# The recurrence's value rows: mixed in time in the first main stage for both directions, and loaded mixed

## The chip, the core and the metric

The kernel runs on one core of a Trainium2 chip. The core has a matrix engine (PE, with its weight loads shown as PEld), a vector engine (DVE), a scalar engine (ACT), a general engine (POOL), a queue that issues transfers (SP) and 16 DMA engines between the chip's memory (HBM) and the core's own (SBUF). Matmuls write into PSUM, eight banks of 128 x 512 numbers. Each engine runs its own instructions in the order in which they stand in its stream, and waits for other engines by semaphores. The metric is the device time of one execution in microseconds. Before the change it is 2432.16 us, the median of three runs (2431.11 to 2433.72).

## The reference, cut to what matters

One layer of a diffusion backbone for 256 latent tokens and 256 context tokens of width 2048. A modulated norm is projected by `w_in`; a bidirectional recurrence (RWKV-7) and a convolution module run on parts of the projection; gates merge both; then come an output projection and 16 routed experts. What the change touches is the mixing in time of the recurrence's inputs:

```python
def _rwkv_direction(P, lp, d):
    ...
    z = z + lp['tok_mu'][d] * (_token_shift(z, direction) - z)
    r, k, v, zw, za = jnp.split(z, ...)
    ...
# in the scan, per token and head
    S = S * w_t - sa * (kk_t * a_t) + v_t^T k_t
# per direction
    bonus = jnp.sum(r * k * _heads(lp['r_k']), axis=-1, keepdims=True) * v
```

For each direction d the rows of r, k and v are a weighted mean of a token and its neighbour, the one before for d = 0 and the one after for d = 1, with a weight for each channel. The value rows v enter the state update and the bonus.

## The kernel before, in words

Tokens lie along the free dimension: 512 columns, 256 of context and then 256 of latents; channels lie on the 128 partitions. The recurrence's 16 heads are eight pairs of 128 channels, and each pair has two directions, so there are 16 units, each a pair in one direction.

The weights come from HBM in pieces of 128 x 512 (`split_w`): SP loads `wraw`, ACT rounds it into `whi`, POOL or DVE takes the rest `wlo`, and PE runs three matmuls (L221 to L223) for each 128 x 128 block. In the first main stage POOL and DVE take `wlo` in turns; in the recurrence's stage POOL takes all.

First main stage (about 165 to 543 us): for each pair, `win_block` projects k, v and r into a PSUM bank, and `out_k`, `out_v` or `out_r` takes it out. The blocks are woven with eight blocks of the convolution (`glu_block`), each with 30 DVE instructions of one tap (L463), with a layer norm after them, and with pieces of the modulation's matmuls. `out_k` copies its bank into a padded tile `P2` (`padded`, L365 to L371: two POOL memsets of the two borders, one ACT copy) of which there are two, then mixes for both directions (`mix`, L373 to L375: ACT scales by one minus the weight, DVE adds the weighted neighbour) and SP stores both results to `kd`. `out_r` does the same with one token stream. `out_v` (L432 to L435) copies the bank as it is and stores it to `vd`, one store.

Recurrence's stage (about 543 to 1320 us): `load_pair` loads the raw value rows of a pair into the padded tile `Pv` (one buffer, two POOL memsets, one load of 256 KB). `rwkv_dir` makes a unit in five segments; segments of up to five units are interleaved. Its first segment loads `km`, `kn`, `rm` and `lw`, and fills the tile `VK` (one buffer): every third block of 64 columns holds mixed value rows (L641 to L644: two ACT and two DVE instructions of 128 x 256), the others hold rows made from `kn` and `rm`. `scores` multiplies blocks of `KB` and `VK` on PE (L729), DVE masks the result into `AT` (L731) and `KM` (L734), `flip` transposes `VK` and `KB` on PE (L740). From `AT`, ACT makes `Ab` (four copies), and from that DVE starts a serial chain of small instructions (L781 to L808) that inverts a triangular block. Value rows are also read for the bonus (L706, L708). Beside the units, pieces of the gates' projections (the fills, L221 to L223 into a bank `big`) and of the modulation (L271) run on PE.

After that come the output projections (to about 1430 us) and the experts (to the end), which are read from HBM in tiles of 2 MB.

The order on each engine is set by a scheduler that places instructions by their priority (the order in the program, with an offset for the fills) and by its own estimate of times. So a change of one instruction moves others, on all engines.

Of the kernel before, what the change touches and what calls it, by code (L numbers as in the profile page):

```python
# [9 lines left out]
F32 = mybir.dt.float32  # L10
F32R = mybir.dt.float32r
AF = mybir.ActivationFunctionType
OP = mybir.AluOpType
# [7 lines left out]
NP = 8  # L21
# [107 lines left out]
def kernel(  # L129
# [6 lines left out]
    PE, DVE, ACT, POOL, SP = nc.tensor, nc.vector, nc.scalar, nc.gpsimd, nc.sync  # L136
# [3 lines left out]
    dram = ctx.enter_context(tc.tile_pool(name="dram", bufs=1, space=bass.MemoryType.DRAM))  # L140
# [4 lines left out]
    def act_copy(o, i, scale=1.0):  # L145
        return ACT.activation(o, i, AF.Copy, scale=scale)  # L146
# [9 lines left out]
    def vec(name, i, n=1):  # L156
        a = _VEC[name][0]
        return V[:, a + i:a + i + n]
# [14 lines left out]
    omu = drv[:, 0:50]  # L173
# [27 lines left out]
    ygd = dram.tile([128, NP, NT], F32, name="ygd")  # L201
    gdr = dram.tile([128, 2, KD, NT], F32, name="gdr")
    kd = dram.tile([128, NP, 2, 2, 512], F32, name="kd")
    vd = dram.tile([128, NP, 512], F32, name="vd")
    nd = dram.tile([NP, 2, 2, 4, 128], F32, name="nd")
    rd = dram.tile([128, NP, 2, NT], F32, name="rd")

# [154 lines left out]
    with tc.tile_pool(name="p1", bufs=1) as p1:  # L362
        if WB1:
            WPS[:] = [[wst] + WB, [p1] + WB1]
        def padded(p, both):  # L365
            n = 2 if both else 1
            P = p1.tile([128, n, 258], F32, name="P%d" % n, bufs=2)
            POOL.memset(P[:, :, 0:1], 0.0)
            POOL.memset(P[:, :, 257:258], 0.0)
            act_copy(P[:, :, 1:257], p.rearrange("p (s t) -> p s t", s=2)[:, 2 - n:2])  # L370
            return P  # L371

        def mix(o, P, d, om, mu):  # L373
            ACT.activation(o, P[:, :, 1:257], AF.Copy, scale=om)
            DVE.scalar_tensor_tensor(o, P[:, :, 2 * d:2 * d + 256], mu, o, op0=OP.mult, op1=OP.add)  # L375

        for d in range(2):
            P = padded(acc0[d], True)
# [51 lines left out]
            kfin.extend([put, get, fin])  # L430

        def out_v(p, acc):  # L432
            t = p1.tile([128, 512], F32, name="vs", bufs=2)
            act_copy(t, acc)
            SP.dma_start(vd[:, p], t)  # L435

        def out_r(p, acc):
            P = padded(acc, False)
# [56 lines left out]

        BIG[:] = ["big", "rw"]
        outs = (out_k, out_v, out_r)
        kfin = []

# [94 lines left out]
    pend, acc = [], [0.0, 1.0]  # L594
# [23 lines left out]
    def rt(name, tag, shape, dt=F32):  # L618
        return rw.tile([128] + list(shape), dt, name=name, tag=tag, bufs=BUF.get(tag, 1))

    def hs(h):
        return slice(64 * h, 64 * h + 64)

    def rwkv_dir(p, d, Pv, bonr, bon, INP):
        c8 = lambda x: x.rearrange("p (c t) -> p c t", t=64)
        cp2 = lambda x: x.rearrange("p (c b) t -> p c b t", b=2)
        i16 = d * 8 + p
        mui = lambda s: 24 * d + 8 * s + p
        mu = lambda s: (omu[:, mui(s):mui(s) + 1], vec("mu", mui(s)))
        VK = rt("VK", "VK", [24, 64])  # L630
        VKv = VK.rearrange("p (c b) t -> p c b t", b=6)
        KB = rt("KB", "KB", [16, 64])
# [4 lines left out]
        SP.dma_start(kn, kd[:, p, d, 1])  # L637
        rm = rt("rm", "rm", [256])
        SP.dma_start(rm, rd[:, p, d])
        om, mv = mu(2)  # L640
        for s in range(2):  # L641
            o = VK[:, 12 * s:12 * s + 12:3]
            ACT.activation(o, c8(Pv[:, s, 1:257]), AF.Copy, scale=om)
            DVE.scalar_tensor_tensor(o, c8(Pv[:, s, 2 * d:2 * d + 256]), mv, o, op0=OP.mult, op1=OP.add)  # L644
        lw = rt("lw", "lw", [2, 128])
        SP.dma_start(lw, lora[p, :, d])
        lwh = rt("lwh", "lwh", [2, 128], F32R)
# [126 lines left out]
        for z, r in quads:  # L774
# [7 lines left out]
                                 op0=OP.mult, op1=OP.add)  # L782
# [4 lines left out]
        for j in range(1, 15):  # L787
            n, m = j, 15 - j
            tmp = rt("tmp", "tmp", [2 * 56])[:, 0:2 * n * m]
            if d == 0:  # L790
# [3 lines left out]
                o = Nv[:, :, j + 1:16, 0:j]  # L794
            else:
# [3 lines left out]
                o = Nv[:, :, 0:j, j + 1:16]  # L799
# [28 lines left out]
        e, o = (0, 32) if d == 0 else (32, 0)  # L828
        pq = c8(bank("sb"))
        for cp, h, c, q in each():  # L830
            a, b, i = 64 * q + e, 64 * q + o, 2 * cp + h
# [7 lines left out]
        for cp, h, c, q in each():  # L839
            a, b, i = 64 * q + e, 64 * q + o, 2 * cp + h  # L840
# [24 lines left out]
        for i, c in enumerate(order):  # L865
            cp, b, j, sl_ = c // 2, c % 2, i % 2, 2 * (i // 2)
            q = 1 - b
            for h in range(2):
                hh_ = h if b == 0 else 1 - h
                tick(0.1)  # L870
                lhs, o = KN[hs(q), cp, hh_], PP[j][hs(hh_)]
# [8 lines left out]
        for j in range(2):  # L880
            DVE.tensor_tensor(PT[:, 2 - j:8 - j:2], PP[j][:, 2 - 2 * j:8 - 2 * j:2], id3, op=OP.add)
            o = RB[:, j::2] if d == 0 else RB[:, 3 - j::-2]
# [29 lines left out]
    INP = rw.tile([128, 16, 32], F32, name="INP")  # L912
    POOL.memset(INP, 0.0)

    def load_pair(p):
        gw = rt("gw", "gw", [128])
        SP.dma_start(gw, g2[:, 128 * p:128 * p + 128])
        bonr = rt("bonr", "bonr", [128])
        POOL.tensor_scalar(bonr, bones, vec("rk", p), -1.0, op0=OP.mult, op1=OP.mult)
        Pv = rt("Pv", "Pv", [2, 258])  # L920
        POOL.memset(Pv[:, :, 0:1], 0.0)
        POOL.memset(Pv[:, :, 257:258], 0.0)
        SP.dma_start(Pv[:, :, 1:257], vd[:, p].rearrange("p (s t) -> p s t", s=2))
        return dict(bon=rt("bon", "bon", [256]), gw=gw, bonr=bonr, Pv=Pv)

    yh, yl = slh, sll

# [6 lines left out]
    def group_norm(p, S):  # L934
        (y0, y1), b0 = S["y"], S["bon"]
        DVE.tensor_tensor(y0, y1, y0, op=OP.add)
        ys = y0
        if dbg is not None and stop == "rwkv":
            SP.dma_start(dbg["y"][p], ys)
            SP.dma_start(dbg["bon"][p], b0)  # L940
        pm = bank(GNB)
        PE.matmul(pm[:, 0:256], bones, ys, start=True, stop=True)
        DVE.scalar_tensor_tensor(ys, pm[:, 0:256], -1.0 / 64, ys, op0=OP.mult, op1=OP.add)
        sq = rt("ysq", "ys", [256])
        ACT.activation(sq, ys, AF.Square)
        PE.matmul(pm[:, 256:512], bones, sq, start=True, stop=True)
        ACT.activation(sq, pm[:, 256:512], AF.Sqrt, scale=1.0 / 64, bias=eps[:, 1:2])
        DVE.reciprocal(sq, sq)
        POOL.tensor_tensor(ys, ys, sq, op=OP.mult)
        DVE.scalar_tensor_tensor(ys, ys, vec("lng", p), b0, op0=OP.mult, op1=OP.add)  # L950
        PE.matmul(pm[:, 0:256], S["gw"], sgl, start=True, stop=True)
        DVE.scalar_tensor_tensor(ys, ys, vec("lnb", p), pm[:, 0:256], op0=OP.add, op1=OP.mult)
        if p < PD:
            SP.dma_start(ygd[:, p, :], ys)
        else:
            act_copy(yh[:, p], ys)
            POOL.tensor_tensor(yl[:, p], ys, yh[:, p], op=OP.subtract)
# [4 lines left out]
    gens = {}  # L962

    def seg(n, i):
        if i >= len(units):
            return
        p, d = units[i]
        if n == 1:
            if d == 0:
                S[p] = load_pair(p)  # L970
            q = S[p]
            gens[i] = rwkv_dir(p, d, q["Pv"], q["bonr"], q["bon"], INP)
        r = next(gens[i])
        if n == 5:
            y = r
            ys = rt("ys", "ys", [256])
            act_copy(ys, y)
            S[p].setdefault("y", []).append(ys)
            if d == 1:
                group_norm(p, S[p])  # L980

    with tc.high_priority(offset=-LOWP):
        for f in early:
            f()
    seg(1, 0)
    seg(2, 0)
    seg(1, 1)
    seg(3, 0)
    seg(2, 1)
# [61 lines left out]
    for k in range(KD):  # L1051
# [13 lines left out]
        with tc.issue_after(a.ins):  # L1065
            if k in XLD:
                q = slice(4 * XLD.index(k), 4 * XLD.index(k) + 4)
# [86 lines left out]
    for s in range(2):  # L1154
        for q in range(4):
            o = xk[:, s, 4 * q:4 * q + 4]
# [153 lines left out]
    for s in range(2):  # L1310
        t = slice(128 * s, 128 * s + 128)
# [70 lines left out]
```

## Time and profile before

The profiled execution took 2433.61 us, 2431.8 us of which is its span from the first to the last instruction; what lies around the span is 1.8 us. It is 1.45 us above the median of the three timed runs.

| engine | busy us in the span | share |
|---|---|---|
| PE | 2006.9 | 83% |
| PEld | 1415.9 | 58% |
| DVE | 1023.9 | 42% |
| ACT | 763.2 | 31% |
| POOL | 650.8 | 27% |

A share over the whole span hides the stages: in the last 1000 us the DMA engines are 0.96 busy with the experts' weights and the other engines wait for them; in the first main stage and the output projections PE is the busiest, and in the recurrence's stage DVE comes close to it. Whatever moves the start of the experts' stage moves the end by as much. A busy PE is not PE at its peak, and the column of the granted clock says at what speed it ran: 1.00 is 2.4 GHz, and a mean below that is a mixture with 1.2 GHz.

### The profile page before, as it was taken

To read this page: it belongs to the slowest core of one execution; us is meant where nothing else is said; L and a number is where in the kernel's file an instruction comes from. 1 tells how busy PE (TensorE), PEld (TensorE's weight loads), DVE (VectorE), ACT (ScalarE), POOL (GpSimd) and SP (SyncE) were. 2 spreads that over 40 slices of the span, in tenths; PEclk is the share of its full clock that TensorE was granted. 3 is DMA by queue.
4 is the path that set the end of the run, shared out by engine and by line. 5 is a ranking of instruction groups with operands and counts; after the bars stand their busy time and mean duration, and the time that the engine had idled before them with its cause. 6 is when DMAs were issued, how large, how long until landed. Compare 5 with 4: busy or idle time off the path is not lost.

```text
span 2431.8 us, 45085 instructions
## 1 busy us (share of the span) xinstructions
PE 2006.9 (83%) x18730; PEld 1415.9 (58%) x18730; DVE 1023.9 (42%) x2029; ACT 763.2 (31%) x1524; POOL 650.8 (27%) x690
## 2 busy tenths in 40 slices
PE   7998999996877989988798996877777777777765
PEld 3787888894755877767678994433333333333332
DVE  2337888426777787665601543211111111111112
ACT  3254333634545565556443541000000000000002
POOL 1342333336433545445445732000000000000002
PEclk9999999998778999999998998888889889888987
DMA  9958666665213334234256887999999999999995
GB/s 384 343 183 271 216 218 233 202 213 181 60 56 109 125 123 139 96 134 152 97 197 198 280 314 303 427 427 428 428 427 427 428 427 429 427 428 427 428 416 221
DMA packets 145932, 669.94 MB, mean 275 GB/s; under 512 B 17344, under 2 KB 40000, under 8 KB 108608
## 3 DMA queue, kind: packets, MB, share of 16 engines
q1 hardware_dynamic: 128208, 455.49, 50.9%
q10 hardware_dynamic: 17520, 211.58, 20.6%
q8 instruction: 147, 2.41, 0.4%
q14 instruction: 57, 0.47, 0.1%
HBM read 647.28 MB, written 19.73 MB: 274 GB/s over the span
## 4 chain that ended last, share of the span: by engine, by line
DMA 31%; PE 20%; DVE 6%; ACT 3%; POOL 2%; issue 2%; SPq 0%; ACTq 0%; DVEq 0%; POOLq 0%
DMA wx<-in_w_gu 18%; DMA wx<-in_w_dn 10%; PE big L1261 2%; PE rw L1224 2%; DMA wraw<-in_w_in 2%; PE p L1293 2%; DVE N L800 1%; PE rw L1253 1%; PE big L221 1%; PE big L223 1%; PE rw L223 1%; PE big L222 1%; PE rw L221 1%; PE rw L222 1%; POOL wlo L217 1%
## 5 line engine op out<-in xcount | busy, mean ns | idle before, releaser
L217 POOL TENSOR_TENSOR wlo<-wraw,whi 128x512 fp32r<-128x512 f32 x292 | 394.4, 1356 | 517.4 <-ACT whi L146 450.0
L1261 PE MATMUL big<-wx,xse 128*32 128x512 f32 x2048 | 300.1, 721 | 160.3 <-DMA wx<-in_w_gu 158.4
L146 ACT ACTIVATE whi<-wraw 128x512 fp32r<-128x512 f32 x428 | 263.4, 627 | 420.2 <-DMA wraw<-in_w_in 130.0
L221 PE MATMUL big<-hh,whi 128*128 128x256 f32 x912 | 272.7, 299 | 13.6 <-ACT whi L146 6.1
L223 PE MATMUL big<-hh,wlo 128*128 128x256 f32 x912 | 271.0, 298 | 10.1 <-POOL wlo L217 9.9
L1261 PEld LDWEIGHTS big<-wx,xse 128*32 128x32 f32 x2048 | 63.8, 121 | 358.9 <-DMA wx<-in_w_gu 183.6
L222 PE MATMUL big<-hl,whi 128*128 128x256 f32 x912 | 268.1, 294 | 0.0
L1237 POOL TENSOR_TENSOR r<-r 128x256 f32<-128x256 f32 x11 | 8.2, 747 | 922.0 <-ACT r L1233 921.6
L221 PEld LDWEIGHTS big<-hh,whi 128*128 128x128 f32 x912 | 181.7, 199 | 40.0 <-issue 17.7
L223 PEld LDWEIGHTS big<-hh,wlo 128*128 128x128 f32 x912 | 181.6, 199 | 23.2 <-POOL wlo L217 14.1
L1274 ACT ACTIVATE th<-big 128x256 f32<-128x256 f32 x16 | 6.1, 384 | 584.9 <-PE big L1261 472.5
L222 PEld LDWEIGHTS big<-hl,whi 128*128 128x128 f32 x912 | 182.1, 200 | 7.4 <-issue 5.8
L1275 DVE SCALAR_TENSOR_TENSOR th<-th,big 128x256 f32<-128x256 f32 x16 | 6.7, 421 | 408.0 <-ACT th L1274 408.0
L1228 DVE SCALAR_TENSOR_TENSOR x<-rw,modT,x 128x256 f32<-128x256 f32 x256 | 111.3, 479 | 142.1 <-PE rw L1224 142.0
L217 DVE TENSOR_TENSOR wlo<-wraw,whi 128x512 fp32r<-128x512 f32 x136 | 112.7, 834 | 131.0 <-ACT whi L146 122.7
L1224 PE MATMUL rw<-oT,ye 128*128 128x256 f32 x512 | 132.4, 403 | 32.5 <-ACT ye L146 31.7
L223 PE MATMUL rw<-hh,wlo 128*128 128x256 f32 x512 | 149.9, 294 | 6.8 <-POOL wlo L217 6.8
L221 PE MATMUL rw<-hh,whi 128*128 128x256 f32 x512 | 150.3, 296 | 1.5 <-ACT whi L146 1.1
L222 PE MATMUL rw<-hl,whi 128*128 128x256 f32 x512 | 149.0, 293 | 0.0
L463 DVE SCALAR_TENSOR_TENSOR cv<-up,hcw,cv 128x256 f32<-128x256 f32 x240 | 144.6, 608 | 9.5 <-ACT cv L461 2.8
L1224 PEld LDWEIGHTS rw<-oT,ye 128*128 128x128 f32 x512 | 95.2, 196 | 85.9 <-ACT ye L146 72.4
L1253 PEld LDWEIGHTS rw<-oh,xk 128*128 128x128 f32 x1024 | 123.2, 194 | 34.2 <-issue 29.1
(359 smaller groups left out, 3901.4 us busy)
## 6 DMA issues: line engine op xcount, KB each, us to landing
wx<-in_w_gu ACTq DMA_DIRECT2D x66, 2048.0 KB, 39.2
wx<-in_w_gu SPq DMA_DIRECT2D x61, 2048.0 KB, 39.3
wm<-in_w_mod SPq DMA_DIRECT2D x96, 1024.0 KB, 7.2
wraw<-in_w_in SPq DMA_DIRECT2D x300, 256.0 KB, 4.2
wx<-in_w_dn ACTq DMA_DIRECT2D x32, 2048.0 KB, 38.6
wx<-in_w_dn SPq DMA_DIRECT2D x31, 2048.0 KB, 38.1
wraw<-in_w_o SPq DMA_DIRECT2D x64, 256.0 KB, 6.1
wraw<-in_w_co SPq DMA_DIRECT2D x32, 256.0 KB, 3.0
```

The source lines that it names most:

```text
L146: return ACT.activation(o, i, AF.Copy, scale=scale)
L217: (POOL if LO[0] < LO[1] else DVE).tensor_tensor(lo, raw, hi, op=OP.subtract)
L221: PE.matmul(o, hi, xh, start=start, stop=False, skip_group_check=True)
L222: PE.matmul(o, hi, xl, start=False, stop=False, skip_group_check=True)
L223: PE.matmul(o, lo, xh, start=False, stop=stop, skip_group_check=True)
L463: DVE.scalar_tensor_tensor(o, up[:, :, j:j + 64], hcw[:, i * KC + j:i * KC + j + 1], o, op0=OP.mult, op1=OP.add)
L800: DVE.tensor_tensor(o, o, tv, op=OP.add)
L1224: PE.matmul(pq[:, 256 * q:256 * q + 256], y[:, 128 * q:128 * q + 128], oT, start=True, stop=True)
L1228: DVE.scalar_tensor_tensor(x, pq[:, 256 * q:256 * q + 256], modT[:, 5, k + q, 0:1], x, op0=OP.mult, op1=OP.add)
L1253: PE.matmul(pxs[:, k], xk[:, s, k], oh[:, s, e], start=(s == 0), stop=(s == 1))
L1261: PE.matmul(pg[32 * j:32 * j + 32, :], xs[:, k, :], w[:, a:a + 512], start=(k == 0), stop=(k == KD - 1))
L1293: PE.matmul(pd[32 * j:32 * j + 32, u], aT[:, 128 * b + 32 * j:128 * b + 32 * j + 32], w[:, 2 * j + b, u], start=(b == 0), stop=(b == 1))
```

## The change

`out_v` now does with the value rows what `out_k` does with the keys: it copies the bank into a padded tile `P2`, mixes for both directions and stores two tiles; `vd` has a place for each direction. `rwkv_dir` loads its direction's mixed rows into a tile `vm` (one buffer) after `rm`, and one ACT copy puts them into every third block of `VK`. The padded tile `Pv`, its memsets and its load are gone, and so are the two ACT and two DVE instructions of each unit.

```diff
-    vd = dram.tile([128, NP, 512], F32, name="vd")
+    vd = dram.tile([128, NP, 2, 512], F32, name="vd")
...
         def out_v(p, acc):
-            t = p1.tile([128, 512], F32, name="vs", bufs=2)
-            act_copy(t, acc)
-            SP.dma_start(vd[:, p], t)
+            P = padded(acc, True)
+            for d in range(2):
+                i = 24 * d + 16 + p
+                t = p1.tile([128, 512], F32, name="vs", bufs=2)
+                mix(t.rearrange("p (s t) -> p s t", s=2), P, d, omu[:, i:i + 1], vec("mu", i))
+                SP.dma_start(vd[:, p, d], t)
...
-    def rwkv_dir(p, d, Pv, bonr, bon, INP):
+    def rwkv_dir(p, d, bonr, bon, INP):
...
-        om, mv = mu(2)
-        for s in range(2):
-            o = VK[:, 12 * s:12 * s + 12:3]
-            ACT.activation(o, c8(Pv[:, s, 1:257]), AF.Copy, scale=om)
-            DVE.scalar_tensor_tensor(o, c8(Pv[:, s, 2 * d:2 * d + 256]), mv, o, op0=OP.mult, op1=OP.add)
+        vm = rt("vm", "vm", [512])
+        SP.dma_start(vm, vd[:, p, d])
+        act_copy(VK[:, 0::3], c8(vm))
...
-        Pv = rt("Pv", "Pv", [2, 258])
-        POOL.memset(Pv[:, :, 0:1], 0.0)
-        POOL.memset(Pv[:, :, 257:258], 0.0)
-        SP.dma_start(Pv[:, :, 1:257], vd[:, p].rearrange("p (s t) -> p s t", s=2))
-        return dict(bon=rt("bon", "bon", [256]), gw=gw, bonr=bonr, Pv=Pv)
+        return dict(bon=rt("bon", "bon", [256]), gw=gw, bonr=bonr)
```

The scheduler's order shows where it now puts these. Lines of the changed kernel are three higher than before up to the recurrence and a few lower behind it.

On SP at the start of the recurrence's stage, before (`gw` and `lw` are small weights, `Pv` the raw value rows, `km`, `kn`, `rm` the rows of unit 0):

```order
L917 DMA gw<-in_g 128x128
L923 DMA Pv<-vd 128x2x256
L635 DMA km<-kd 128x512
L637 DMA kn<-kd 128x512
L639 DMA rm<-rd 128x256
L646 DMA lw<-in_lora 128x256
```

and now:

```order
L916 DMA gw<-in_g 128x128
L636 DMA km<-kd 128x512
L638 DMA kn<-kd 128x512
L640 DMA rm<-rd 128x256
L642 DMA vm<-vd 128x512
L645 DMA lw<-in_lora 128x256
```

The value rows of the first unit are issued fourth of the four loads, where they were first.

On DVE in the middle of the recurrence's stage, before (around the unit whose value rows are mixed at about 850 us; `AT` are the masked scores of one unit, `INP` and `N` the start of its serial chain):

```order
L674 SCALAR_TENSOR_TENSOR Wp<-dp,C 128x520
L674 SCALAR_TENSOR_TENSOR Wy<-di,C 128x520
L682 SCALAR_TENSOR_TENSOR Wy<-di,Wy 128x520
L731 TENSOR_TENSOR AT<-rw,C 128x4x64 x2
L644 SCALAR_TENSOR_TENSOR VK<-Pv,V,VK 128x4x64 x2
L692 TENSOR_TENSOR KB<-kp,Wy 128x4x2x64
L692 TENSOR_TENSOR KB<-ta,Wy 128x4x128
L781 SCALAR_TENSOR_TENSOR INP<-Ab,C 128x8x16
```

and now, at the start of the chain of a unit at the same place:

```order
L821 TENSOR_TENSOR T_9464<-T,sb 128x256
L823 STREAM_TRANSPOSE TT<-T_9464 128x256
L730 TENSOR_TENSOR AT<-rw,C 128x4x64 x2
L780 SCALAR_TENSOR_TENSOR INP<-Ab,C 128x8x16
L782 SCALAR_TENSOR_TENSOR INP<-Ab,C,INP 128x8x16
```

The pair of mixing instructions between the masked scores and the start of the chain is gone, and here the two `KB` products stand elsewhere too.

On DVE in the first main stage, now (`vs` are mixed value rows, `cv` the convolution's taps, `wlo` the rest of a weight piece); before, the two rows with `vs` were not there:

```order
L466 SCALAR_TENSOR_TENSOR cv<-up,hcw,cv 128x256 x5
L375 SCALAR_TENSOR_TENSOR vs<-P_2567,V,vs 128x512
L466 SCALAR_TENSOR_TENSOR cv<-up,hcw,cv 128x256
L375 SCALAR_TENSOR_TENSOR vs<-P_2567,V,vs 128x512
L466 SCALAR_TENSOR_TENSOR cv<-up,hcw,cv 128x256 x3
L217 TENSOR_TENSOR wlo<-wraw,whi 128x512
```

The mixing stands in the middle of a convolution's chain of taps.

## Rows read from the trace of the kernel before

**Rows 1.** Busy time of the engines by stretch, granted clock, DMA.

```profile
core 0: us, PE busy (x) PEld busy (x) DVE busy (x) ACT busy (x) POOL busy (x), PEclk, DMA share, GB/s
...
200.00:440.00 240.00, 222.65 (x1726) 196.57 (x1724) 201.01 (x343) 95.38 (x169) 81.10 (x87) 0.96 0.68 229
440.00:543.00 103.00, 99.97 (x811) 92.52 (x810) 35.01 (x59) 49.09 (x94) 33.38 (x33) 0.97 0.67 219
...
580.00:820.00 240.00, 186.31 (x2756) 152.84 (x2752) 183.07 (x346) 121.49 (x262) 106.78 (x126) 0.79 0.26 82
820.00:1060.00 240.00, 220.24 (x3301) 177.82 (x3301) 171.12 (x356) 145.30 (x314) 118.59 (x130) 0.95 0.41 135
...
1240.00:1320.00 80.00, 67.81 (x489) 58.79 (x488) 6.44 (x11) 30.56 (x58) 44.75 (x37) 0.87 0.65 208
1320.00:1430.00 110.00, 106.72 (x910) 103.52 (x911) 55.00 (x77) 56.54 (x108) 66.69 (x65) 1.00 0.82 279
```

**Rows 2.** Waits of the engines from 200 to 440 us: total, times, longest.

```profile
POOL up L456 <- DVE cv L463: 20.3, 6, 7.1
```

**Rows 3.** Waits of the SP queue, same stretch.

```profile
SPq L214 <- DVE wlo L217: 68.6, 36, 6.2
...
SPq L401 <- DVE km L375: 7.6, 4, 3.2
```

**Rows 4.** The mixing's DVE line: duration in ns, min/median/max, first and last start.

```profile
L375 DVE SCALAR_TENSOR_TENSOR km<-P,V,km x16: 735/745/1186, 160.0 to 516.4; 128x512 f32<-128x512 f32 x16
```

**Rows 5.** The mixing's ACT line, same columns.

```profile
L374 ACT ACTIVATE km<-P,drv x16: 709/715/733, 159.2 to 515.6; 128x512 f32<-128x512 f32 x16
```

**Rows 6.** The page's line of ACT's plain copy of 128 x 512.

```profile
L146 ACT ACTIVATE whi<-wraw 128x512 fp32r<-128x512 f32 x428 | 263.4, 627 | 420.2 <-DMA wraw<-in_w_in 130.0
```

**Rows 7.** What reads or writes the tile Pv.

```profile
L643 ACT ACTIVATE VK<-Pv,drv x32: 492/497/512, 546.8 to 1144.4; 128x256 f32<-128x256 f32 x32
L644 DVE SCALAR_TENSOR_TENSOR VK<-Pv,V,VK x32: 472/774/1396, 547.4 to 1145.0; 128x256 f32<-128x256 f32 x32
...
DMA to landing us min/median/max: 3.2/3.5/7.2
```

**Rows 8.** DVE's timeline: value rows followed by a wait (start us, us).

```profile
575.74 1.13 DVE L644 SCALAR_TENSOR_TENSOR VK<-Pv,V,VK 128x256 f32<-128x256 f32 x2
578.30 0.92 DVE L781 SCALAR_TENSOR_TENSOR INP<-Ab,C 128x128 f32<-128x128 f32 x1 [1.43 <-ACT Ab L146]
...
1144.57 0.87 DVE L644 SCALAR_TENSOR_TENSOR VK<-Pv,V,VK 128x256 f32<-128x256 f32 x2
1147.23 0.93 DVE L781 SCALAR_TENSOR_TENSOR INP<-Ab,C 128x128 f32<-128x128 f32 x1 [1.79 <-ACT Ab L146]
```

**Rows 9.** DVE's timeline: value rows with no wait behind them.

```profile
655.43 2.15 DVE L644 SCALAR_TENSOR_TENSOR VK<-Pv,V,VK 128x256 f32<-128x256 f32 x2
...
850.05 2.16 DVE L644 SCALAR_TENSOR_TENSOR VK<-Pv,V,VK 128x256 f32<-128x256 f32 x2
...
854.37 0.81 DVE L781 SCALAR_TENSOR_TENSOR INP<-Ab,C 128x128 f32<-128x128 f32 x1
...
962.98 1.80 DVE L644 SCALAR_TENSOR_TENSOR VK<-Pv,V,VK 128x256 f32<-128x256 f32 x2 [0.18 <-ACT VK L643]
```

**Rows 10.** ACT's timeline at the same place as the middle rows of that.

```profile
850.41 1.68 ACT L146 ACTIVATE Ab<-AT 32x256 f32<-32x256 f32 x4
```

**Rows 11.** SP's timeline at the start of the recurrence's stage.

```profile
543.05 0.43 SPq L923 DMA_DIRECT2D Pv<-vd  x1
543.52 0.47 SPq L635 DMA_DIRECT2D km<-kd  x1
...
544.63 0.43 SPq L639 DMA_DIRECT2D rm<-rd  x1
```

**Rows 12.** ACT's timeline there.

```profile
546.81 0.91 ACT L643 ACTIVATE VK<-Pv,drv 128x256 f32<-128x256 f32 x2 [2.52 <-DMA Pv<-vd]
```

More of the change, by code (lines that the diff above doesn't have):

```diff
@@ L627, in rwkv_dir @@
         i16 = d * 8 + p
-        mui = lambda s: 24 * d + 8 * s + p
-        mu = lambda s: (omu[:, mui(s):mui(s) + 1], vec("mu", mui(s)))
         VK = rt("VK", "VK", [24, 64])
@@ L971, in seg @@
             q = S[p]
-            gens[i] = rwkv_dir(p, d, q["Pv"], q["bonr"], q["bon"], INP)
+            gens[i] = rwkv_dir(p, d, q["bonr"], q["bon"], INP)
         r = next(gens[i])
```

## The prediction

> **What bounds the kernel now.** I read first the busy time by stretch, to see which stages the change touches and who is short there; then the waits of the first main stage; then the instructions that are removed and those like the added ones; and last the timelines of DVE, ACT and SP at the places where the removed ones stood.
>
> The stretches [rows 1] show three regimes. From 200 to 440 us, where the convolution's taps run, PE is busy for 222.7 of 240 us at a clock of 0.96, and DVE for 201.0 of 240, or 84%. From 440 to 543 us PE is busy for 100.0 of 103 and DVE for only 35.0. In the recurrence's stage DVE is busy for 183.1 of 240 us in the first part (580 to 820 us), while PE stands at 186.3 with a clock of 0.79; in the second part (820 to 1060 us) PE has 220.2 of 240 at 0.95 and DVE 171.1. So the first part belongs to the serial chain over DVE, ACT and PE, and in the second PE is close to being the limit. What lies behind (the output projections at a clock of 1.00, then the experts' weights) is not touched, and passes on what comes before it.
>
> The change moves work from the stage in which DVE sets the pace half of the time to one in which PE sets it. The question is how much of what goes was on the path, and how much of what comes finds room.
>
> **The first main stage: added.** Eight pairs of heads, two directions each: 16 DVE instructions of 745 ns [rows 4] are 11.9 us, 16 ACT instructions of 715 ns [rows 5] are 11.4 us; the copy out of the bank stays, 16 small memsets and eight more stores come. ACT is busy for 40% and 48% of the two stretches [rows 1] and hides its part. Of DVE's, the value rows of pairs 0 and 1 come before the taps begin, those of pairs 5 to 7 in the stretch with DVE at a third; PE's work covers them. Those of pairs 2, 3 and 4 are 6 x 0.745 = 4.5 us in the stretch that is 84% full. There DVE does reach PE: POOL stands 20.3 us at a memset that waits for taps [rows 2] with weight splits queued behind it, and SP stands 68.6 us at loads whose buffer DVE's half of the splits has not released [rows 3]. I take 4.5 x 0.84 = **+3.8 us**. The low end is 0: nothing goes from this stage that could gain. The high end adds SP: a store of mixed rows waits for DVE, and a key store did so for 7.6 / 4 = 1.9 us [rows 3] with weight loads queued behind it; six such stores are 11.4 us, together 15.9 us.
>
> **The recurrence's stage: its start.** The first unit's value rows were issued at 543.05 us, and ACT waited 2.5 us for them before it did anything else [rows 11, 12]. Now they go fourth, where `rm` went at 544.63 [rows 11], 1.6 us later; the copy behind is 0.28 us shorter (next part). On ACT the rounding of `lw` and the unit's first activations are queued behind it: **+1.3 us**, between 0 and that.
>
> **DVE's part, removed.** 32 instructions, of 472 to 1396 ns [rows 7]. After the first unit there are 15 pairs. In seven, DVE waits afterwards for something else, mostly for `Ab` from ACT, 1.43 us in the first and 1.79 us in the last of them [rows 8]: these are worth nothing. In eight pairs DVE goes on without a wait, from 655.43 to 962.98 us [rows 9]. There the pair takes up to 2.16 us, but a pair that nothing disturbs takes 0.87 [rows 8]. Of the time as it stands, less what the next wait would give back (at 850 us `Ab` is ready at 852.1 [rows 10] and the chain starts at 854.4 [rows 9], so all 2.16 count), the eight make 11.8 us; undisturbed they make 8 x 0.87 = 7.0 us. I take the lower, since what stretches a pair is still there when the pair is gone and meets the next instruction: **-7.0 us**, between 0 and -11.8.
>
> The Trainium skill (GPSIMD Engine Reference, "Specifications" and "Key points") says that POOL shares its SBUF interface with VectorE and that they contend when VectorE has two SBUF inputs. The mixing instruction has two such inputs, and so has the `KB` product behind it. By that rule the time over 0.87 us belongs to POOL's work, which stays, and the gain would be 7.0; without it, 11.8. The spread of one shape from 472 to 1396 ns agrees with it [rows 7].
>
> **ACT's part.** Two copies of 128 x 256, 0.91 us as a pair [rows 12], become one of 128 x 512; the nearest row is a plain copy of that size from SBUF, 627 ns [rows 6], so 0.28 us less for each unit. It counts where the chain waits for `Ab` behind it, five of the seven places above: **-1.4 us**, between 0 and 16 x 0.28 = -4.5.
>
> **Loads, POOL, the end of the stage.** A unit's load of 256 KB lands in 3.5 us [rows 7]; there are 16 for 8, in a stage whose DMA share is 0.26 to 0.41 [rows 1]. The buffer is free as soon as the copy before has run, a unit earlier than it is needed: nothing, as long as SP comes to it in time (a rival). 16 memsets on POOL go: nothing. The scheduler has also moved fills: behind the last unit's group norm 78 groups of three matmuls of gates stood before, 71 now. From 1240 to 1320 us 489 matmuls took 80 us [rows 1], 0.164 us each, so 21 fewer are **-3.4 us**; the low end is 0, since the seven stand inside the recurrence now.
>
> **Sum:** 3.8 + 1.3 - 7.0 - 1.4 - 3.4 = -6.7 us. On the profiled execution of 2433.6 that is 2426.9; this execution lies 1.45 us above the median of the timed runs, so I forecast 2425.5 us.
>
> **Rivals.**
> - *No change, PE paces it.* Four of the eight pairs lie after 820 us, where PE is 92% busy at 0.95 [rows 1]; DVE's freed time there is spent waiting for PE, and fills put forward cost what they save at the end. Then 3.8 + 1.3 - 3.5 - 1.4 = +0.2, or 2432.4. For it speaks that row; against it that this clock still leaves gaps, which a shorter chain fills.
> - *Slower, SP's queue in the first stage.* The stores of mixed value rows stand in front of weight loads. The high end: 15.9 + 1.3 - 7.0 - 1.4 = +8.8, or 2441.0. It decides once PE's idle time from 200 to 440 us, now 17.4 us, grows by more than the 10.5 us that the rest gives, to about 28. For it speaks SP's 68.6 us; against it that SP waits for buffers most of that time anyway, so that a store's wait partly lies in the same time.
> - *Slower, the mixed rows come late.* If SP, standing at other waits, issues `vm` only when `VK` is free, ACT stands up to 3.5 us with `Ab` queued behind: at five places 17.5, so 17.5 + 3.8 + 1.3 - 7.0 = +15.6, or 2447.8. Against it: a whole unit of cover.
> - *Faster than forecast.* The disturbed time goes too: -11.8 in place of -7.0, so -11.5, or 2420.7.
>
> **How the numbers follow.** Forecast 0.33, faster still 0.12, no change 0.30, SP's queue 0.19, late rows 0.06. A change of less than 0.2% (4.9 us) can't be told from none here; so faster 0.45, within 0.2% 0.30, slower 0.25. With the best ends of all terms (-11.8 - 4.5 - 3.4 = -19.7) the time would be 2412.5, with the worst 2449. The range is 2414 to 2441: it reaches past the larger gain below and to SP's price above, and leaves out the late rows and the rims. The forecast's own range, with the DVE term between -3.5 and -11.8, is 2420 to 2429. That the scheduler orders everything anew is in no term; it is why the range is not narrower.
>
> **What would show it.** Right: DVE from 200 to 440 us at about 205 us and the start of the recurrence's stage about 4 us later than 543; the copy into `VK` at about 0.63 us with no wait for a load except in the first unit; DVE's line of the value rows gone from the recurrence's stage, the eight chains starting a good 0.8 us earlier after `AT`; that stage about 10 us shorter. Wrong: the recurrence's stage as long as before with PE's busy time up in its second half (no change); SP's waits at stores of `vd` of 10 us and more, with PE idle from 200 to 440 us (slower); waits of ACT for `vm` (late rows).

## The result, and the profile after

The changed kernel took 2469.41 us, the median of 4 runs (2463.76 to 2474.34); the kernel before took 2431.64 us beside it (4 runs, 2423.98 to 2433.72). The ratio is 1.0156, 95% interval 1.0134 to 1.0178: slower by 38 us, outside the predicted range. The profiled execution of the changed kernel has a span of 2466.5 us, against 2431.8.

The same stretches as in [rows 1], after:

```profile
200.00:440.00 240.00, 223.57 (x1716) 192.20 (x1717) 209.75 (x353) 102.94 (x181) 83.46 (x95) 0.97 0.71 236
440.00:543.00 103.00, 97.81 (x818) 90.12 (x817) 41.35 (x66) 52.76 (x101) 34.42 (x39) 1.00 0.70 227
580.00:820.00 240.00, 191.26 (x2835) 158.61 (x2833) 167.96 (x356) 126.65 (x269) 102.69 (x119) 0.79 0.27 84
820.00:1060.00 240.00, 195.35 (x2947) 161.14 (x2947) 135.25 (x294) 118.77 (x257) 101.15 (x101) 0.86 0.34 108
1060.00:1240.00 180.00, 150.31 (x2061) 121.54 (x2060) 109.82 (x221) 94.61 (x200) 87.55 (x85) 0.91 0.40 131
1240.00:1320.00 80.00, 68.16 (x820) 56.42 (x819) 9.24 (x16) 35.13 (x74) 41.61 (x35) 0.96 0.62 205
1320.00:1430.00 110.00, 101.69 (x808) 98.71 (x809) 44.90 (x63) 52.57 (x99) 73.22 (x67) 0.94 0.76 238
```

Read it against [rows 1] line by line; the line that is not shown there, for the kernel before, is

```profile
1060.00:1240.00 180.00, 152.74 (x2249) 125.42 (x2245) 97.80 (x204) 89.12 (x195) 80.84 (x75) 0.91 0.37 122
```

The two lines of the first main stage are those of before but for DVE, which has 8.7 and 6.3 us more to do, and ACT, which has 7.6 and 3.7; PE does 2534 matmuls there where it did 2537. From 580 to 820 us the changed kernel is as good as before. Most of the loss stands in one line, 820 to 1060 us: PE did 2947 matmuls where it did 3301, its clock is 0.86 instead of 0.95, and every other engine did less too. From 1060 to 1240 us it did another 188 fewer. From 1240 us on PE makes up for work left behind (820 matmuls for 489).

What the change itself was to do, it did. Two groups of rows of the changed kernel, by tile: the mixing in the first stage (durations in ns, min/median/max, then first and last start), and the copy into `VK`:

```profile
L374 ACT ACTIVATE vs<-P,drv x16: 707/717/727, 163.7 to 530.2; 128x512 f32<-128x512 f32 x16
L375 DVE SCALAR_TENSOR_TENSOR vs<-P,V,vs x16: 741/747/1822, 164.5 to 531.1; 128x512 f32<-128x512 f32 x16
...
L146 ACT ACTIVATE VK<-vm x16: 613/632/634, 548.4 to 1181.0; 128x512 f32<-128x512 f32 x16
```

The waits of the SP queue in the recurrence's stage, from 543 to 1260 us (total, times, longest), show one at a load that was not there before, that of `vm`:

```profile
SPq L214 <- POOL wlo L217: 244.6, 91, 15.8
SPq L573 <- DVE gtt L572: 58.0, 12, 11.9
SPq L642 <- ACT VK L146: 53.6, 9, 17.4
```

One buffer holds `vm`, so the next unit's load stands at the head of SP's queue until the unit before has been copied, and weight loads stand behind it. That was the first suspect. But SP had waits of nearly the same total before, at the load of `kn`, which the profile puts down to POOL's instruction that makes other rows of `VK` from `kn`, and that one has nearly gone; before, then now:

```profile
SPq L637 <- POOL VK L695: 42.0, 8, 15.0
```

```profile
SPq L638 <- POOL VK L694: 2.4, 2, 2.2
```

So much of the wait at `vm` took the place of another. ACT's copy of `vm` stood behind a load only in the first unit (3.7 us, which the profile puts down to `gw`).

The places where the time goes are best found by the start of each unit's serial chain, the first instruction of DVE into `INP` (L780; L781 before). Before, units 8 to 16 start at 854, 892, 929, 967, 1002, 1050, 1090, 1147 and 1182 us. After, they start at 838, 888, 922, 990, 1030, 1092, 1130, 1184 and 1222 us. The changed kernel is 17 us ahead at the eighth unit, and then has gaps of 50, 68, 62 and 54 us where before has mostly 35 to 48, and 57 once.

The widest gap, 922 to 990 us, in the changed kernel: stretches inside its first half, with the columns of [rows 1], then PE's and DVE's timelines (start us, us, ...).

```profile
922.00:930.00 8.00, 6.48 (x104) 5.75 (x104) 7.25 (x20) 7.04 (x19) 2.20 (x3) 1.00 0.01 2
930.00:936.00 6.00, 0.00 (x0) 0.00 (x0) 5.41 (x16) 0.00 (x0) 0.96 (x1) 0.63 0.37 109
936.00:945.00 9.00, 8.66 (x180) 7.44 (x184) 1.29 (x5) 1.91 (x5) 0.00 (x0) 0.50 0.01 2
945.00:958.00 13.00, 13.00 (x175) 12.11 (x167) 4.77 (x8) 9.57 (x18) 7.63 (x7) 0.99 0.32 98
```

```profile
929.35 0.27 PE L894 MATMUL gn<-Z,PT 64*64 64x64 f32 x2
936.34 0.85 PE L812 MATMUL sb<-T,X 32*32 32x32 f32 x44 [6.71 <-DVE T L807]
...
957.70 0.50 PE L288 MATMUL p<-C,wm 128*128 128x1 f32 x4
...
959.67 0.40 PE L653 MATMUL p<-zs,lwh 128*128 128x512 f32 x1
```

```profile
935.84 0.45 DVE L807 STREAM_TRANSPOSE T<-TT 128x256 f32<-128x256 f32 x1
...
958.24 0.16 DVE L290 TENSOR_TENSOR modT<-p,V 128x4 f32<-128x4 f32 x1 [0.88 <-PE p L288]
965.76 1.80 DVE L673 TENSOR_TENSOR_SCAN Wp<-dp,C 128x520 f32<-128x520 f32 x1 [7.36 <-ACT dp L667]
```

PE first has nothing to do for 6.7 us while DVE runs a unit's chain, since the next instruction in its list is the product of that chain (L812). Then it has some 20 us of gate matmuls, during which DVE is busy for 4.8 of 13 us and then stands for 7.4, because the next unit's first matmul (L653) comes only behind them and behind a modulation finish (L288) in the same bank `p1`. In this gap chain and fills stand one after the other where they could lie beside each other. PE's first 9 us after the pause also run at a clock of 0.50.

The scheduler's PE list shows the same without any time in it. Between one unit's first product of 32x32 blocks and the next unit's stand this many gate matmuls, from the eighth gap to the fifteenth, and behind the last:

```
before  78  93  70 122 131  61 160  83 | 514
after   98  35 227  57 188  27 168 111 | 481
```

So three theories. **SP:** the wait of the `vm` load holds up weight loads, and fills and units with them. **Bank:** modulation finishes in `p1` hold up the units' first matmuls. **Order:** the scheduler made a new list for all engines, and this one lays chains and fills badly; what the change does to the value rows has no other part in it.

### The profile page after: what moved, and what is told of

Read it like the earlier page. It is cut to its first block, busy times and chain, and to the rows that moved or that the text cites. A ratio compares the mean times of both kernels' runs of the same rounds, so it can differ in the third digit from the quotient of the medians.

```text
span 2466.5 us, 45093 instructions
## 1 busy us (share of the span) xinstructions
PE 2018.0 (82%) x18730; PEld 1421.7 (58%) x18730; DVE 1007.2 (41%) x2013; ACT 770.0 (31%) x1524; POOL 654.4 (27%) x690
## 3 DMA queue, kind: packets, MB, share of 16 engines
q1 hardware_dynamic: 129488, 459.68, 50.8%
## 4 chain that ended last, share of the span: by engine, by line
DMA 30%; PE 25%; DVE 7%; ACT 3%; issue 2%; POOL 2%; SPq 0%; ACTq 0%; DVEq 0%; POOLq 0%
DMA wx<-in_w_gu 16%; DMA wx<-in_w_dn 11%; PE rw L1219 2%; PE big L223 2%; DVE N L799 2%; PE big L1256 2%; PE big L221 2%; PE big L222 2%; PE p L1288 2%; PE rw L223 2%; PE rw L221 2%; PE rw L222 1%; PE rw L1248 1%; DMA wraw<-in_w_in 1%; DVE tmp L796 1%
## 5 line engine op out<-in xcount | busy, mean ns | idle before, releaser
L217 DVE TENSOR_TENSOR wlo<-wraw,whi 128x512 fp32r<-128x512 f32 x136 | 118.1, 873 | 112.2 <-ACT whi L146 100.3
```

The costliest lines, as they stand in the source:

```text
L217: (POOL if LO[0] < LO[1] else DVE).tensor_tensor(lo, raw, hi, op=OP.subtract)
```

## Experiments: the queue, the bank, and parts of the change alone

**1. `vm` loaded by ACT.** In the changed kernel:

```
-        SP.dma_start(vm, vd[:, p, d])
+        ACT.dma_start(vm, vd[:, p, d])
```

> The changed kernel with one edit: the load of the mixed value rows (vm) is issued by ScalarE instead of by the DMA queue of SyncE (SP). In the changed kernel SP stood 53.6 us in nine waits of that load, behind which the loads of the weights are queued. Theory SP (the loads of the weights, held up behind that wait, come late, and with them the pieces of the gates and of the modulation that stand in TensorE's stream between two units): the wait is gone from SP's list, DMA in 820 to 860 us is back near 150 GB/s, the finish of the modulation that stands before the ninth unit ends near 836 us instead of 854 us, and the time is 2422 to 2437 us. Theory bank (the new order puts the modulation's finish, in the one bank p1, ahead of the next unit's first matmul; SP has no part in it): the gaps of 50 to 68 us between units stay, 2455 to 2475 us. Theory order (the scheduler made another list, and any other list is as good or bad by chance): anything from 2425 to 2470 us, with gaps at other places.

Measured: 2455.39 us, ratio to before 1.0106 (1.0078 to 1.0135). The wait is gone from SP's list, and most of the loss stays, with gaps of 62, 49 and 56 us. The wait at `vm` can't be the main cause by itself, but the list is another one here too (170, 80, 110, 87, 140 gate matmuls from the eighth gap on), and the wait at the load of `kn` is back at 26.5 us.

**2. The modulation's finish in another bank.**

```
         def finish():
-            pt = bank("p1").rearrange("p (n s) -> p n s", s=2)
+            pt = bank("sb").rearrange("p (n s) -> p n s", s=2)
```

> The changed kernel with one edit: the modulation's finish takes the PSUM bank sb instead of p1, the bank that the first matmul of every unit needs too. Theory bank: the first matmul of a unit no longer waits for the finish, the units' chains start every 36 to 42 us throughout, 2425 to 2440 us. Theory SP: the pieces come late as before, 2455 to 2475 us, the wait at the vm load stays at 40 to 60 us. Theory order: 2425 to 2470 us, without regard to the bank.

Measured: 2445.51 us, ratio 1.0047 (1.0026 to 1.0069). Better, but a gap of 72 us remains, next to 221 gate matmuls in the list. Not decided between bank and order.

**3. Before, without DVE's mixing.**

```
-            DVE.scalar_tensor_tensor(o, c8(Pv[:, s, 2 * d:2 * d + 256]), mv, o, op0=OP.mult, op1=OP.add)
```

> The kernel before with only VectorE's sixteen times two mixing instructions left out (the second half of the mixing is not computed); loads, buffers and queues stay as they were. All theories agree that VectorE's 23.8 us off the recurrence's stage give something if nothing else comes in: 2418 to 2428 us by the prediction's term of 7.0 us and a share for what else waits on it. Theory order: the list is made anew here too, so it may as well be 2440 us or more, with gaps between units as in the changed kernel.

Measured: 2437.32 us, ratio 1.0032 (1.0015 to 1.0048). Taking 32 instructions off DVE and adding nothing made the kernel slower. The gain that all theories had granted did not come.

**4. Before, raw value rows loaded once for each unit.** The four lines that make and load `Pv` move from the pair's loads into the unit's:

```
     def rwkv_dir(p, d, bonr, bon, INP):
...
+        Pv = rt("Pv", "Pv", [2, 258])
+        POOL.memset(Pv[:, :, 0:1], 0.0)
+        POOL.memset(Pv[:, :, 257:258], 0.0)
+        SP.dma_start(Pv[:, :, 1:257], vd[:, p].rearrange("p (s t) -> p s t", s=2))
```

> The kernel before with only the load of the value rows changed: the raw rows (Pv) are loaded once for each unit, sixteen times, into the one buffer, instead of once for a pair of units; the mixing stays in the recurrence. Theory SP: the second load of a pair waits at the head of SP's queue for the mixing of the unit before, as vm does in the changed kernel (40 us or more on SP's list), and the time goes up by 1 to 2%, 2450 to 2480 us. Theory bank and theory mixing (the loss comes from what was taken off the recurrence, not from the load): 2428 to 2440 us. Theory order: 2425 to 2470 us.

Measured: 2453.40 us, ratio 1.0092 (1.0065 to 1.0118), with 50.8 us of SP's waits at that load. By itself this spoke for SP; experiments 13 and 14 come back to it.

## Experiments: the same instructions in another order

The fills are laid out by a line that places the modulation's pieces among the gates' (`at`), with a start inside each column's share (0.1) and a spread (`MSP`, 0.15). Changing a number there changes no instruction, only the list. The numbers tried were chosen by the lists that they give, by how evenly the gate matmuls lie between units.

**5 and 6. The changed kernel with an even list.**

```
-MSP = 0.15
+MSP = 0.5
```

```
-        at = lambda i: (i // m + 0.1 + MSP * (i % m + 0.5) / m) / nc_
+        at = lambda i: (i // m + 0.8 + MSP * (i % m + 0.5) / m) / nc_
```

> The changed kernel with one number changed: the four pieces of a modulation column are spread over half of their share of the fill list (MSP 0.5) instead of 0.15 of it. No instruction is added, removed or changed; only the order of the fills, and so the scheduler's lists, differ. In the changed kernel's PE list the gate matmuls between one unit's first 32x32 matmuls and the next unit's are 227, 57, 188, 27, 168, 111 from the eleventh unit on (before: 122, 131, 61, 160, 83 from its twelfth on, none over 160); in this one they are 75, 155, 36, 143, 86 at the end and never over 155. Theory order (the loss is the uneven list): gaps between units of at most 58 us, the last group norm near 1275 us instead of 1308, 2425 to 2442 us. Theory SP (the vm load's wait in SP's queue, which stays): 2455 to 2475 us. Theory bank (the modulation's finish ahead of the units in bank p1, which stays): 2450 to 2475 us.

> The changed kernel with one number changed: each modulation column starts at 0.8 of its share of the fill list instead of 0.1. No instruction is added, removed or changed. Gate matmuls between units in the PE list: never over 101 up to the twelfth unit, then 50, 200, 81, 125. Theory order: one gap of over 55 us instead of three, 2425 to 2445 us. Theories SP and bank: 2450 to 2475 us.

Measured: 2428.77 us, ratio 0.9983 (0.9970 to 0.9997), and 2431.79 us, ratio 1.0002 (0.9989 to 1.0015). All of the 38 us are gone. SP's wait of the `vm` load is still there in the fifth (543 to 1260 us), as is the finish in bank `p1`:

```profile
SPq L642 <- ACT VK L146: 37.6, 11, 8.7
```

PE at a chain's product in the fifth kernel: 2.00 us of waiting where the changed kernel had 6.71, since fills stand ahead of it.

```profile
921.68 1.06 PE L271 MATMUL big<-wm,slp 128*32 128x512 f32 x8 [1.11 <-DMA wm<-in_w_mod]
...
924.75 0.39 PE L812 MATMUL sb<-T,X 32*32 32x32 f32 x24 [2.00 <-DVE T L807]
```

That is one place. PE's longest waits from 840 to 1240 us (total, times, longest), in the changed kernel and then in the fifth, don't single out this product:

```profile
PE gn L894 <- DVE PT L880: 23.3, 3, 8.8
PE sb L812 <- DVE T L807: 13.0, 2, 6.7
```

```profile
PE rw L728 <- DVE KB L691: 24.1, 5, 9.2
PE sb L812 <- DVE T L807: 12.4, 5, 6.1
```

So what is shown is that the list costs the time; that it does so at every gap in the way of the one from 922 to 990 us is not shown.

**7 and 8. The kernel before with an uneven list:** the same line, with a start of 0.3 and of 0.2.

> The kernel before with one number changed: each modulation column starts at 0.3 of its share of the fill list instead of 0.1. No instruction is added, removed or changed, and none of the value rows' change is in it. Gate matmuls between units in the PE list become uneven as in the changed kernel: 30, 66, 206, 43, 231, 85. Theory order: gaps of 55 to 68 us at these two places, 2445 to 2470 us. Theories SP and bank as causes that the change brought: no vm load, so 2426 to 2438 us.

> The kernel before with one number changed: each modulation column starts at 0.2 of its share of the fill list instead of 0.1. No instruction is added, removed or changed. Gate matmuls between units in the PE list: 129, 14, 231, 78, 109, 45, 217, 61, the most uneven of the lists tried. Theory order: 2450 to 2475 us, with gaps of over 60 us at 231 and 217. Theories SP and bank: 2426 to 2438 us.

Measured: 2450.14 us, ratio 1.0070 (1.0046 to 1.0094), and 2457.12 us, ratio 1.0104 (1.0084 to 1.0124). Without a trace of the change, the kernel before loses up to two thirds of what the change lost, and at the foretold places: the gaps with 206 and 231 gate matmuls are 66 and 61 us wide in the seventh. This is the mirror of 5 and 6, and together they show the order to be the cause. The recurrence's stage in two halves (columns as in [rows 1]), for the kernel before, the changed one, the fifth and the seventh in turn:

```profile
543.00:840.00 297.00, 232.18 (x3237) 189.85 (x3237) 209.93 (x403) 148.90 (x316) 135.33 (x161) 0.81 0.33 103
840.00:1240.00 400.00, 354.86 (x5251) 286.82 (x5250) 255.77 (x520) 224.65 (x487) 194.06 (x198) 0.93 0.39 129
```

```profile
543.00:840.00 297.00, 237.83 (x3392) 195.94 (x3392) 188.28 (x395) 153.95 (x322) 132.45 (x152) 0.81 0.33 105
840.00:1240.00 400.00, 325.66 (x4609) 265.48 (x4606) 234.82 (x488) 200.72 (x429) 181.20 (x178) 0.88 0.37 119
```

```profile
543.00:840.00 297.00, 243.05 (x3500) 195.89 (x3500) 200.40 (x397) 159.89 (x335) 146.12 (x163) 0.86 0.37 117
840.00:1240.00 400.00, 340.48 (x5048) 274.86 (x5045) 243.28 (x495) 211.11 (x459) 188.50 (x184) 0.92 0.40 128
```

```profile
543.00:840.00 297.00, 243.57 (x3496) 199.26 (x3500) 207.41 (x419) 162.39 (x343) 141.24 (x164) 0.85 0.35 109
840.00:1240.00 400.00, 332.00 (x4804) 267.49 (x4802) 248.65 (x501) 204.65 (x444) 185.57 (x189) 0.88 0.37 119
```

The sum of PE's two counts is the measure: by 1240 us the four kernels had done 8488, 8001, 8548 and 8300 matmuls, and their spans are 2431.8, 2466.5, 2423.1 and 2451.1 us. In these 697 us PE had no matmul for 110.0, 133.5, 113.5 and 121.4 us; so of the 34.7 us between the first two spans 23.5 are PE's waits, and the rest fits its lower clock.

**9 to 12. More lists:** the changed kernel with starts of 0.9 and 1.0, the kernel before with a spread of 0.05, and the third experiment's kernel with a start of 0.3.

> The changed kernel with one number changed: each modulation column starts at 0.9 of its share of the fill list instead of 0.1. Its PE list is the most even of all that were compared: from 31 to 127 gate matmuls between one unit's first 32x32 matmuls and the next unit's. Theory order: no gap between units above 52 us, the last group norm by 1262 us, 2412 to 2430 us, below the kernel before by 0.2 to 0.7%; the mixing taken out of the recurrence then shows its worth. Rival, the mixing is worth nothing (TensorE paces the stage whatever the list): 2428 to 2436 us, no difference from before.

> The changed kernel with one number changed: each modulation column starts at 1.0 of its share of the fill list instead of 0.1. Gate matmuls between units: 46 to 146, and 48 at the last. Theory order: 2415 to 2432 us. Rival, the mixing is worth nothing: 2428 to 2436 us.

> The kernel before with one number changed: the four pieces of a modulation column stand within 0.05 of its share of the fill list instead of 0.15. Its list is as even as that of the kernel before (27 units' worth the same, never over 140 gate matmuls between units against 160). Theory order: 2425 to 2436 us, like before. If the kernel before owes its time to one lucky list rather than to an even one: 2440 us or more.

> The kernel before without VectorE's mixing (the second half of the mixing is not computed), with the start of each modulation column at 0.3 of its share instead of 0.1. Its list is more even than that of the same kernel with the mixing at 0.3 (never over 136 gate matmuls between units, against 231). Theory order: 2420 to 2436 us, at least 14 us under the 2450 us of the kernel with the mixing at 0.3. If the start at 0.3 itself costs the time, whatever the list: 2440 to 2450 us.

Measured: 2432.91 us, ratio 1.0001 (0.9988 to 1.0014); 2424.79 us, 0.9975 (0.9960 to 0.9990); 2423.59 us, 0.9969 (0.9955 to 0.9982); 2431.24 us, 1.0004 (0.9989 to 1.0019). The ninth kernel has the most even list and gains nothing by it: there theory order promised too much, and "the mixing is worth nothing" gave the time. The tenth kernel's 2424.79 us lies in the range of theory order and under that of its rival, but the eleventh, which still has the mixing, is as fast, a little under the 2425 to 2436 us expected of it. The best list of the kernel before and the best of the changed kernel end 1.2 us apart, with overlapping intervals.

**13 and 14. Experiment 4 with other lists** (start 0.8; spread 0.5).

> The kernel of the fourth experiment (before, with the raw value rows loaded once for each unit) with the start of each modulation column at 0.8 of its share of the fill list instead of 0.1: the same instructions and the same wait of SP, another list (16 to 132 gate matmuls between units). Theory order: 2422 to 2438 us. Theory SP (the second load into the one buffer costs the 0.9% of the fourth experiment): 2445 to 2460 us.

> The kernel of the fourth experiment with the pieces of a modulation column spread over 0.5 of its share of the fill list instead of 0.15 (22 to 151 gate matmuls between units, and 576 behind the last, more than in any other). Theory order: 2425 to 2442 us. Theory SP: 2445 to 2460 us.

Measured: 2436.70 us, ratio 1.0016 (0.9998 to 1.0034), and 2438.89 us, ratio 1.0031 (1.0012 to 1.0049), with SP's waits at the load still 35.8 and 31.9 us. Most of the 0.9% of experiment 4 was its list. What is left, 0.16 and 0.31%, is no more than lists differ by; the kernel before was not run with these two settings, so whether any of it is the waits' is not shown.

## Why the prediction was wrong, step by step

**The step that failed** is the sentence "That the scheduler orders everything anew is in no term", and with it the only place where order was counted, the -3.4 us for fewer gate matmuls behind the last group norm. The count looked at the end of the list and not at the 15 gaps between units, where the list had changed most. Its price can be put together from the two traces: the last unit's chain starts at 1222.07 us instead of 1182.12, 40.0 us later, and 33 fewer gate matmuls stand behind it (481 for 514), at the prediction's 0.164 us 5.4 us. That makes +34.5, and the spans differ by 34.7. The same sum (start of the last chain plus 0.164 us for each gate matmul behind it) gives the spans of all fourteen experiments within 9 us, so the agreement to 0.2 us is partly luck. The sum says where the loss lies, between the first chain and the last; that the order put it there is what experiments 5 to 8 show.

**The first main stage, +3.8 us: nothing.** DVE's ten instructions more between 200 and 440 us, six of them the mixing as foretold, found room; the stage behind starts with the same instruction of POOL (the memset of `INP`) at 542.73 us, before at 542.71. The rival on SP's queue fell too: its waits at stores of `vd` are 13.9 us in all from 100 to 543 us, over the 10 us that the prediction named as its sign, but PE from 200 to 440 us is busier than before, 223.57 for 222.65 us.

**The start, +1.3 us:** right in kind. The copy into `VK` ran at 548.41 instead of 546.81, and the first chain started at 581.00 instead of 578.30 us, 2.7 us later.

**DVE's part, -7.0 us, and ACT's, -1.4:** not seen in the time, though the copy into `VK` took 632 ns as priced. The 17 us by which the changed kernel leads at the eighth unit are mostly work put off: before that point its list has 315 gate matmuls between units and before's has 399, and 84 at 0.164 us are 13.8 of the 16.7 us. That price is an average of a stretch in which PE also waits; at the 0.118 us at which gate matmuls follow each other in the changed kernel from 945.51 to 947.28 us they are 9.9. The 2.9 to 6.8 us that are left, and the 2.7 of the late start made up, are all that seven units can have gained, and the second half gave them back.

Part of the time freed on DVE became waiting for ACT: in front of the sixteen chains DVE stood waiting for `Ab` 22.4 us before (10 times), 31.0 us in experiment 3 (11 times) and 34.8 us in the changed kernel (14 times). The prediction's count of eight pairs in full was too high by its own rule. Two of them, at 655.43 and 692.83 us, come right behind the `AT` from which `Ab` is made, and DVE waits for that `Ab` six instructions later:

```profile
663.63 0.45 DVE L781 SCALAR_TENSOR_TENSOR INP<-Ab,C 128x128 f32<-128x128 f32 x1 [2.28 <-ACT Ab L146]
...
700.63 0.94 DVE L781 SCALAR_TENSOR_TENSOR INP<-Ab,C 128x128 f32<-128x128 f32 x1 [3.67 <-ACT Ab L146]
```

With the mixing left out and nothing added, two lists gave 1.0032 and 1.0004; the changed kernel's four retuned lists gave 0.9975 to 1.0002, the four of the kernel before 0.9969 to 1.0104. So the no-change rival had the size of what the mixing itself is worth, and it rightly said that freed time becomes waiting. That the waiting is for PE, as it said, is not shown: PE was not busier from 820 to 1060 us, the sign that was named, but had 195.35 us in the changed kernel and 212.78 in the fifth for 220.24 before. Whether there is a loss or gain of up to 0.3% can't be told from lists that differ. The rule of the Trainium skill (GPSIMD Engine Reference, "Specifications" and "Key points") that was to decide between 7.0 and 11.8 us decided nothing, as neither came.

**Loads and SP: "nothing, as long as SP comes to it in time".** SP came in time: ACT's copy never waited for a load after the first unit. But the load held SP itself for 53.6 us, which the prediction had not seen, in part in place of the wait at `kn`: it asked who waits for the load and not what waits behind it. The price turned out small (experiments 5, 6, 13, 14).

Left open: by which rule the scheduler arrives at 227 gate matmuls in one gap. And the counts between units are not all: experiments 1 and 4 have no gap over 170 and still lost about 1%, experiment 3 has a list like before's and lost 0.3%.

## What to carry to other kernels

Where a scheduler orders a kernel, an edit is two changes, the edit and a new list, and here the second was worth up to 38 us and the first nothing that could be measured. Before a forecast, count in both lists how the filling work lies between the steps of the serial chain, along the whole stage and not at its end; and before a verdict, run each version with a few orders of the same instructions and compare the best with the best. Here that also gave the fastest kernel: one number in the placing of the fills, in the kernel before (experiment 11, 0.9969).

## What the runs showed of the chip

In the changed kernel a pause of PE cost more than its length. PE stood still from 929.6 to 936.3 us; its granted clock was 1.00 in the 8 us before and 0.50 in the 9 us after, and 0.99 again from 945 us on (the four stretches above), so a pause of 6.7 us was followed by 9 us at the lower of the two levels, 1.2 GHz. The clock of the whole stretch from 840 to 1240 us fits this: 0.88 with the uneven lists (the changed kernel and the seventh), 0.93 and 0.92 with the even ones (before and the fifth).

Runs of one program spread more than a median of three shows: twelve runs of experiment 10 lie between 2417.45 and 2437.85 us, 0.8% apart, so that effects of 0.2% needed ten runs and more; the interval of ten runs of experiment 5 is 0.27% wide.
